# Seven raw weight tiles with nine loads ahead, and one set of activation buffers instead of two

## The chip, the cores and the metric

The kernel runs on one core of a Trainium2 chip. TensorE (PE) multiplies, VectorE (DVE) and ScalarE (ACT) work elementwise, SyncE (SP) issues nearly all DMA transfers, GpSimd (POOL) does little. The metric is the device time of one execution in microseconds (us); the time before is a median of three runs.

## What is computed

A decoder trunk of two layers over 256 tokens of width 2048, all in float32. The parts that matter here, from the reference:

```python
for layer in range(DEPTH):
    if layer % 2 == 0:
        mix = hybrid_mixer(rms_norm(x, ...), ...)     # state-space heads and stick-breaking attention
    else:
        mix = multiscale_pool(rms_norm(x, ...), ...)  # trailing means of 2/4/8/16 tokens, a map per group, bias, scale
    x = x + mix
    x = x + sq_relu_mlp(rms_norm(x, ...), mlp_w_up[layer], mlp_w_down[layer])

def sq_relu_mlp(h, w_up, w_down):
    u = jax.nn.relu(h @ w_up)
    return (u * u) @ w_down        # 2048 -> 8192 -> 2048
```

## The kernel before

**The list of weights.** `plan()` (L48) writes down all matrix products as units in a fixed order: the input projection of layer 0, its output projection, the MLP of layer 0, the four groups of the pooling layer, the MLP of layer 1. A unit is cut into steps; a step is one load of up to 512 KB of weights, two tiles of 128x512 or four of 128x256. The weights lie in device memory in the order of the steps.

**From load to matmul.** Each step goes through `load` (L198), which issues the DMA on SP's queue into a `raw` tile, and `split` (L215), in which ACT writes `hi`, the weights rounded to the matmul's float32r type (L235), and DVE writes `lo`, the rest (L236). A product is the sum of three matmuls: `hi` times the two halves of the activations, and `lo` times the high half. There are four `raw` tiles, four `hi` and four `lo`. `feed` (L239) keeps the loads six steps and the splits three steps ahead of the step whose matmuls are written next.

**The MLP.** It runs in four blocks of 2048 hidden columns. For block 0, eight `up` units make the squared activations `u`; for blocks 1 to 3, four `up` units make the first half of the columns, and the second half is made by two units, `sa` and `sb`, that use seven products for a two-by-two block product (Strassen's scheme). Their 20 steps are laid by `plan()` among the 32 steps of the `down` units of the block before, from due numbers (L94). For `sb`, DVE first combines the raw tiles of two steps in place (L222 to L225). The sums of activations that the seven products need, `sop`, are made by `gen_sop` (L691) once a layer, eight tiles of them, and are kept until the last `sb` of the layer. The seven products are added and squared in `gen_s` (L735), and the result is turned into place by `to_ring` (L286).

**Where things lie.** Fourteen slots of 8 KB per partition (`slot(i)`) hold normed inputs, mixer outputs, `u` and constants by turns. `u_base` (L788) says in which four slots a block's `u` lies; the blocks of a layer alternate between two sets. `t4` tiles, eight of them, hold short-lived work of the mixer and the pooling layer, and `sop`. The constants of the pooling layer (window matrix, bias, scale) are loaded in `finish` (L839 to L852) after the first `down` unit of the last block of layer 0, into slots 4 to 7, from SP's queue; the bias is added to the residual stream by `add_bias` (L761), and `gen_win` (L766) adds the pooled groups.

**The order.** The program is written in one order by the loop over steps and by small generators that are advanced a tick at a time (`lane`, `lane2`). The tile framework then orders each engine's instructions: it can move one ahead of its place in the program where its inputs and its tile are free, and a new tile of a name waits until the readers of the old one are through. On the chip each engine runs its own list in order.

Of the kernel before, what the change touches and what calls it, by code (L numbers as in the profile page):

```python
# [11 lines left out]
F32R = mybir.dt.float32r  # L12
# [4 lines left out]
P = 128  # L17
# [21 lines left out]


X_EARLY = ((0, 14), (1, 2), (1, 6), (1, 10))
AHEAD_LOAD = 6
WARM = 2
PAD, TURN = 24, 56
AHEAD_SPLIT = 3
# [83 lines left out]
def tile_trunk(ctx: ExitStack, tc: tile.TileContext, x_in, xt_in, w_all, prm_in,  # L129
# [11 lines left out]
    def new(tag, shape, dt=F32, bufs=1, p=sb):  # L141
        count[0] += 1
        return p.tile(shape, dt, tag=tag, name=f"{tag}_{count[0]}", bufs=bufs)

    def slot(i, shape=(P, 2, 4, T), dt=F32R):
        return new(f"st{i}", list(shape), dt)

    def ev():
        return new("ev", [P, MT, 512], bufs=3)

    def t4(n, dt=F32):
        return new("t4", [P, 1088], dt, bufs=8)[:, :n]

    def bank():
        return new("bg", [P, 512], bufs=4, p=ps_bg)
# [1 line left out]
    def v3(ap, a, b):  # L157
        return ap.rearrange("p (a b) -> p a b", a=a, b=b)
# [23 lines left out]
    def load_x(q):  # L182

        m, c = q // 2, slice(D // 2 * (q % 2), D // 2 * (q % 2) + D // 2)
        if q == 0:
            x_sb[:] = [slot(12 + m, (P, D), F32) for m in range(MT)]
        nc.sync.dma_start(x_sb[m][:, c], x_in[m * P : m * P + P, c])
# [10 lines left out]
    def load(i):  # L198
        u, k, tiles, off = steps[i]
        n, nk = units[u]["n"], len(tiles)  # L200
        raw = v3(new("raw", [P, 1024], bufs=4)[:, : nk * n], nk, n)
        if u == 0:
            nc.sync.dma_start(
                xt[k // 8][:, k % 8 : k % 8 + nk, :],
                xt_in[k * P : (k + nk) * P, :].rearrange("(k p) n -> p k n", p=P))
        nc.sync.dma_start(
            raw, w_all[off : off + P * nk * n].rearrange("(p k n) -> p k n", p=P, n=n))
        raws[i] = raw
        if u == 0 and k == 8:
            nc.sync.dma_start(cst, cst_in)  # L210
            nc.sync.dma_start(row, row_in.partition_broadcast(P))
        if (u, k) in X_EARLY:
            load_x(X_EARLY.index((u, k)))
# [25 lines left out]
    def feed(i):  # L239
        while done["load"] < min(len(steps), i + 1 + AHEAD_LOAD):  # L240
            load(done["load"])
            done["load"] += 1
        while done["split"] < min(len(steps), i + 1 + AHEAD_SPLIT):
            split(done["split"])
            done["split"] += 1
# [62 lines left out]
    def spread(name):  # L308

        r = rs[name]  # L310
        dg = v3(t4(2 * P), MT, P)
        for m in range(MT):
            dve.tensor_scalar(dg[:, m], ident, r[:, m : m + 1], None, ALU.mult)
        yield
        b = bank()
        for m in range(MT):
            pe.matmul(b[:, m * P : (m + 1) * P], ones, dg[:, m], start=True, stop=True)
        o = new("rrow", [P, T], bufs=2)
        dve.tensor_copy(o, b[:, :T])
        rs[name, "row"] = o  # L320
# [9 lines left out]
    def norm_chunk(name, c, tiles, slot0, gain):  # L330
        if c == 0:
            rs[name, "ss"] = new("ss", [P, MT, 4], bufs=2)
        ss = rs[name, "ss"]
        junk = t4(512)
        for m in range(MT):
            act.activation(junk, x_sb[m][:, 512 * c : 512 * c + 512], AF.Square,
                           accum_out=ss[:, m, c : c + 1])
        if c == 3:
            s = new("sum", [P, MT], bufs=2)
            dve.tensor_reduce(s, ss, AX.X, ALU.add)  # L340
            r = new("rstd", [P, MT], bufs=2)
            power(r, s, 1.0 / D)
            rs[name] = r
        yield
        yield
        dst = slot(slot0 + c)
        yield from to_ring(lambda m: x_sb[m][:, 512 * c : 512 * c + 512], tiles, 4 * c, dst, gain)
        if c == 3 and name != "pool":
            yield from spread(name)
# [10 lines left out]
    def turn(e, n):  # L360

        yield
        yield
        xT = v3(t4(n * 259), n, 259)
        for h in range(n // 2):
            b = v3(bank(), 2, T)
            for c in range(2):
                for m in range(MT):
                    k = 2 * h + c
                    pe.transpose(b[:, c, m * P : (m + 1) * P], e[:, m, k * P : (k + 1) * P], ident)  # L370
            act.activation(xT[:, 2 * h : 2 * h + 2, 3:], b, AF.Copy)
            yield
        return xT
# [317 lines left out]
    def gen_sop(layer):  # L691


        for p in range(KT // 2):
            t, c = hM[layer][2 * p]
            e = ev()
            a, s = v3(e[:, 0], 2, T), v3(e[:, 1], 4, P)
            dve.tensor_tensor(a, t[:, 0, c : c + 2].bitcast(F32), t[:, 1, c : c + 2].bitcast(F32),
                              ALU.add)
            a11, a21, a12, a22 = (a[:, i, h * P : h * P + P] for i in range(2) for h in range(2))  # L700
            dve.tensor_tensor(s[:, 0], a21, a22, ALU.add)
            dve.tensor_tensor(s[:, 2], a11, a21, ALU.subtract)
            dve.tensor_tensor(s[:, 1], s[:, 0], a11, ALU.subtract)
            dve.tensor_tensor(s[:, 3], a12, s[:, 1], ALU.subtract)
            yield
            o = t4(1024, F32R).rearrange("p (a b c) -> p a b c", a=2, b=4)
            act.activation(o[:, 0], s, AF.Copy)
            dve.tensor_tensor(o[:, 1], s, o[:, 0].bitcast(F32), ALU.subtract)
            sop[layer, p] = o
            yield  # L710
            yield
# [74 lines left out]
        yield  # L786

    def u_base(layer, b):  # L788
        return ((4, 8), (0, 4))[layer][b % 2]

    def finish(u, ps):
        d = units[u]
# [62 lines left out]
        elif kind == "pool":  # L855
            need(lambda: "pool" in rs)
            w = [v3(t4(1024, F32R), MT, 512) for _ in range(2)]
            r = rs["pool"]
            for m in range(MT):
                rm = r[:, m : m + 1]  # L860
                act.activation(w[0][:, m], ps[:, m], AF.Copy, scale=rm)
                dve.scalar_tensor_tensor(w[1][:, m], ps[:, m], rm, w[0][:, m].bitcast(F32),
                                         ALU.mult, ALU.subtract)
            lane.append(gen_win(arg, w))
        elif kind == "up":
            layer, b, i = arg
            name = f"mlp{layer}"
            need(lambda: (name, "row") in rs)
            e = ev()
            ea, eb = v3(e[:, 0], 2, T), v3(e[:, 1], 2, T)  # L870
            add_halves(ea, ps)
            dve.scalar_tensor_tensor(ea, ea, 0.0, row2(name), ALU.max, ALU.mult)
            lane.append(gen_u(b, i, ea, eb, u_base(layer, b)))
            if (b, i) == (0, 0):
                lane2.append(gen_sop(layer))
        elif kind == "sa":

            a = sev["a"] = new("att_b", [P, 3, 512])
            p1, p2, p3 = (sps.pop(q) for q in (1, 2, 3))
            act.activation(a[:, 2], p1, AF.Copy)  # L880
            act.activation(a[:, 1], p3, AF.Copy)
            dve.tensor_tensor(a[:, 0], a[:, 2], p2, ALU.add)
        elif kind == "sb":
            lane.append(gen_s(*arg, u_base(*arg)))
# [42 lines left out]
    for i, (u, k, tiles, _) in enumerate(steps):  # L927
        d = units[u]
        n, nk, src, k0, n2 = d["n"], d["nk"], sources[d["src"]], d["k0"], len(tiles)
# [10 lines left out]
        if u not in accs:  # L940
            accs[u] = ps_main.tile([P, MT, 512], F32, tag="acc", name=f"acc_{u}")
            if d["kind"] == "up" and d["arg"][2] == 0:
                b = d["arg"][1]
# [11 lines left out]
        for kk in range(n2):  # L955
            t, c = src[k0 + k + kk]
# [89 lines left out]
```

## Time and profile before

| what | before |
|---|---|
| median of three runs | 2184.68 us (2181.84 to 2185.71) |
| profiled execution, its own time | 2179.63 us |
| span of its instructions | 2177.8 us |
| PE busy, idle | 2160.8 us, 17.0 us |
| weight load on PE busy | 1816.5 us |
| DVE busy | 1552.5 us |
| ACT busy | 1191.5 us |
| moved by DMA | 454.32 MB, mean 209 GB/s |

Busy times are sums over the span; different stages have different limits, so they are read stage by stage. A matmul's end is modelled, and matmuls overlap, so the time between two starts says more than the time of one. A row of a group gives engine, operation, out<-in with sizes, count, then busy time and mean, then the idle time of the engine ahead of it and what ended it. A row of waits gives who waited for whom, the sum, the number and the longest.

### The profile page before, as it was taken

Reading aid. Unit: us, or ns where it says so; the run is one execution under the profiler, and the core shown is the slowest. Engines: PE = TensorE matmul, PEld = TensorE weight load, DVE = VectorE, ACT = ScalarE, POOL = GpSimd, SP = SyncE. Lnnn points to the kernel's source line nnn. Section 1 sums busy time; section 2 is a strip of 40 time slices with the busy share of each in tenths; the row PEclk is TensorE's granted clock in tenths of the full one; section 3 lists DMA queues with packets and bytes.
Section 4 is the critical chain, followed back from the end, with each engine's and each line's share of the span. In section 5 each row is a group of like instructions: output and inputs, shape, how many; then the busy total and the mean of one; then the engine's idle time right before and its main releaser. Section 6 shows DMA issues by size and latency. Waiting matters only on the chain.

```text
span 2177.8 us, 28400 instructions
## 1 busy us (share of the span) xinstructions
PE 2160.8 (99%) x10613; PEld 1816.5 (83%) x10613; DVE 1552.5 (71%) x1908; ACT 1191.5 (55%) x1399; POOL 21.5 (1%) x21
## 2 busy tenths in 40 slices
PE   9999999999999999999999999999999999999999
PEld 7888888888888888788878878888887887888888
DVE  6988756656555586886886787578778777768754
ACT  7665456665644465455455455456554654654543
POOL 0000000000000000000000000000000000000000
PEclk9999999999999999999999999999999999999999
DMA  8665555555656567766776776655677676677664
GB/s 303 202 205 165 165 184 163 176 165 172 205 187 190 176 200 239 225 230 220 239 240 206 247 257 232 184 174 162 207 242 240 204 250 231 215 242 232 222 202 146
DMA packets 129002, 454.32 MB, mean 209 GB/s; under 512 B 14496, under 2 KB 17248, under 8 KB 128608
## 3 DMA queue, kind: packets, MB, share of 16 engines
q1 hardware_dynamic: 128000, 451.36, 64.5%
q8 instruction: 83, 1.36, 0.3%
q10 hardware_dynamic: 864, 1.15, 0.2%
q14 instruction: 55, 0.45, 0.1%
HBM read 450.32 MB, written 2.13 MB: 208 GB/s over the span
## 4 chain that ended last, share of the span: by engine, by line
PE 89%; DMA 5%; DVE 4%; ACT 1%; issue 1%; DVEq 0%; ACTq 0%; SPq 0%
PE acc L969 52%; PE acc L961 16%; PE acc L963 9%; PE bg L732 8%; DMA raw<-w_all 5%; DVE lo L236 2%; PE bg L294 1%; ACT hi L235 1%; DVE raw L224 1%; DVE raw L223 1%; PE bg L522 1%; DVE raw L225 0%; PE bg L579 0%; PE bg L669 0%; PE bg L614 0%
## 5 line engine op out<-in xcount | busy, mean ns | idle before, releaser
L235 ACT ACTIVATE hi<-raw 128x1024 fp32r<-128x1024 f32 (+2 forms) x846 | 878.7, 1048 | 905.2 <-PE acc L969 442.6
L236 DVE TENSOR_TENSOR lo<-raw,hi 128x1024 fp32r<-128x1024 f32 (+2 forms) x846 | 1012.8, 1205 | 446.4 <-ACT hi L235 422.1
L969 PE MATMUL acc<-hi,st 128*128 128x512 f32 (+2 forms) x3840 | 1165.0, 386 | 1.8 <-ACT hi L235 1.8
L969 PEld LDWEIGHTS acc<-hi,st 128*128 128x128 f32 x3840 | 710.1, 188 | 142.9 <-ACT hi L235 3.7
L969 PE MATMUL acc<-lo,st 128*128 128x512 f32 (+2 forms) x1920 | 736.3, 385 | 1.3 <-DVE lo L236 1.1
L961 PE MATMUL acc<-st,hi 128*128 128x512 f32 x1568 | 552.3, 394 | 0.0
L963 PE MATMUL acc<-st,lo 128*128 128x256 f32 x1568 | 441.7, 282 | 0.0
L969 PEld LDWEIGHTS acc<-lo,st 128*128 128x128 f32 x1920 | 360.6, 188 | 75.6 <-DVE lo L236 3.3
L961 PEld LDWEIGHTS acc<-st,hi 128*128 128x128 f32 x1568 | 294.3, 188 | 62.0 <-issue 1.4
L963 PEld LDWEIGHTS acc<-st,lo 128*128 128x128 f32 x1568 | 296.3, 189 | 2.0 <-issue 1.2
L732 PE MATMUL bg<-hi,t 128*128 128x512 f32 x384 | 119.2, 392 | 0.0
L732 PE MATMUL bg<-hi,st 128*128 128x512 f32 x288 | 88.8, 390 | 0.0
L732 PE MATMUL bg<-lo,t 128*128 128x512 f32 x192 | 77.3, 403 | 8.1 <-DVE lo L236 8.1
L732 PEld LDWEIGHTS bg<-hi,t 128*128 128x128 f32 x384 | 71.3, 188 | 15.9 <-ACT hi L235 2.1
L222 DVE TENSOR_TENSOR raw<-raw 128x512 f32<-128x512 f32 x48 | 33.2, 692 | 45.2 <-DMA raw<-w_all 45.1
L732 PEld LDWEIGHTS bg<-hi,st 128*128 128x128 f32 x288 | 54.1, 188 | 10.4
L732 PEld LDWEIGHTS bg<-lo,t 128*128 128x128 f32 x192 | 36.0, 187 | 25.8 <-DVE lo L236 17.0
L832 DVE TENSOR_TENSOR st<-st,acc 128x512 f32<-128x512 f32 (+1 forms) x74 | 46.4, 668 | 13.8 <-PE acc L969 13.8
L732 PE MATMUL bg<-lo,st 128*128 128x512 f32 x144 | 56.0, 389 | 0.0
L223 DVE TENSOR_TENSOR raw<-raw,raw 128x512 f32<-128x512 f32 x48 | 33.2, 692 | 23.5 <-DMA raw<-w_all 23.3
L282 ACT ACTIVATE st<-bg,prm 128x256 fp32r<-128x256 f32 x64 | 28.4, 467 | 23.9 <-DVE st L283 22.8
L325 DVE TENSOR_TENSOR ev<-acc,ev 128x512 f32<-128x512 f32 x40 | 27.4, 685 | 11.6 <-ACT ev L324 11.6
(190 smaller groups left out, 1067.8 us busy)
## 6 DMA issues: line engine op xcount, KB each, us to landing
raw<-w_all SPq DMA_DIRECT2D x818, 512.0 KB, 3.9
raw<-w_all SPq DMA_DIRECT2D x20, 256.0 KB, 2.9
st<-x_in SPq DMA_DIRECT2D x8, 512.0 KB, 5.1
st<-scr SPq DMA_DIRECT2D x8, 512.0 KB, 6.6
raw<-w_all SPq DMA_DIRECT2D x8, 288.0 KB, 4.2
st<-prow_in SPq DMA_DIRECT2D x2, 1024.0 KB, 7.1
st<-xt_in SPq DMA_DIRECT2D x6, 256.0 KB, 6.9
st<-pmat_in SPq DMA_DIRECT2D x1, 768.0 KB, 7.0
```

What stands on the lines that cost most here:

```text
L222: dve.tensor_tensor(raw[:, 0], raw[:, 1], raw[:, 0], ALU.subtract)
L223: dve.tensor_tensor(raw[:, 1], two[:, 0], raw[:, 1], ALU.subtract)
L224: dve.tensor_tensor(two[:, 0], two[:, 0], raw[:, 0], ALU.subtract)
L235: act.activation(hi, raw, AF.Copy)
L236: dve.tensor_tensor(lo, raw, hi.bitcast(F32), ALU.subtract)
L282: act.activation(dst[:, 0, c], ps, AF.Copy, scale=gain)
L325: dve.tensor_tensor(dst, ps[:, :, :T], dst, ALU.add)
L732: pe.matmul(sps[q], st[h], w[:, j], start=p == 0 and w is hi and h == 0, stop=p == KT // 2 - 1 and w is lo)
L832: dve.tensor_tensor(x_sb[m][:, cs], x_sb[m][:, cs], ps[:, m, : d["n"]], ALU.add)
L961: pe.matmul(ps[:, f].rearrange("p (h t) -> p h t", h=2), hi[:, kk, fs], t[:, :, c], start=first, stop=False)
L963: pe.matmul(ps[:, f, :T], lo[:, kk, fs], t[:, 0, c], start=False, stop=last)
L969: pe.matmul(ps[:, m, :n], t[:, h % 2, c, m * P : (m + 1) * P], (hi, hi, lo)[h][:, kk], start=first and h == 0, stop=last and h == 2)
```

## The change

Four edits, in one diff:

- `raw` has seven tiles instead of four, and loads are written nine steps ahead instead of six.
- `t4` has five tiles of 1036 columns instead of eight of 1088.
- `sop` no longer takes a `t4` tile for each of its eight pairs; two pairs share one slot, slots 8 to 11 in layer 0 and 4 to 7 in layer 1.
- `u` lies in one set of four slots in all blocks of a layer, slots 4 to 7 in layer 0 and 0 to 3 in layer 1, where two sets alternated.

```diff
-AHEAD_LOAD = 6
+RAWS, AHEAD_LOAD = 7, 9
...
     def t4(n, dt=F32):
-        return new("t4", [P, 1088], dt, bufs=8)[:, :n]
+        return new("t4", [P, 1036], dt, bufs=5)[:, :n]
...
-        raw = v3(new("raw", [P, 1024], bufs=4)[:, : nk * n], nk, n)
+        raw = v3(new("raw", [P, 1024], bufs=RAWS)[:, : nk * n], nk, n)
...
-            o = t4(1024, F32R).rearrange("p (a b c) -> p a b c", a=2, b=4)
+            if p % 2 == 0:
+                dst = slot((8, 4)[layer] + p // 2, (P, 2, 2, 4, P))
+            o = dst[:, p % 2]
             act.activation(o[:, 0], s, AF.Copy)
...
     def u_base(layer, b):
-        return ((4, 8), (0, 4))[layer][b % 2]
+        return (4, 0)[layer]
```

## The prediction

> **What bounds the kernel now.** I read the page first (busy shares, costly groups), then the table of waits, then sums over stretches of time, then single instructions in two places.
>
> ```profile
> span 2177.8 us, 28400 instructions
> PE 2160.8 (99%) x10613; PEld 1816.5 (83%) x10613; DVE 1552.5 (71%) x1908; ACT 1191.5 (55%) x1399; POOL 21.5 (1%) x21
> raw<-w_all SPq DMA_DIRECT2D x818, 512.0 KB, 3.9
> ```
> TensorE (PE) has work in all but 17.0 us of the span. No edit here removes a matmul, so the most there is to win is these gaps and the little that a broken rhythm costs around them. Where they lie:
>
> ```profile
> 0.00:15.00 15.00, 11.70 (x37) 7.25 (x38) 8.46 (x16) 9.94 (x17) 0.31 (x5) 1.00 0.87 302
> 15.00:860.00 845.00, 845.00 (x4211) 714.64 (x4210) 571.36 (x801) 486.57 (x598) 19.82 (x14) 1.00 0.60 191
> 865.00:961.00 96.00, 93.81 (x412) 75.49 (x412) 77.78 (x86) 47.34 (x47) 0.00 (x0) 1.00 0.70 231
> 1040.00:1135.00 95.00, 93.76 (x414) 76.03 (x414) 78.02 (x86) 47.28 (x47) 0.00 (x0) 1.00 0.70 234
> 1214.00:1308.00 94.00, 92.96 (x413) 75.96 (x412) 78.18 (x87) 47.67 (x47) 0.00 (x0) 1.00 0.75 252
> 1600.00:1694.00 94.00, 92.67 (x409) 75.03 (x408) 77.17 (x86) 46.73 (x47) 0.00 (x0) 1.00 0.72 237
> 1773.00:1869.00 96.00, 94.37 (x416) 76.46 (x415) 78.82 (x88) 47.32 (x48) 0.00 (x0) 1.00 0.70 234
> 1948.00:2044.00 96.00, 94.08 (x418) 76.64 (x417) 78.75 (x88) 47.91 (x48) 0.00 (x0) 1.00 0.72 233
> 1418.00:1440.00 22.00, 22.00 (x102) 18.20 (x101) 13.60 (x16) 10.98 (x16) 0.00 (x0) 1.00 0.59 188
> 1440.00:1452.00 12.00, 12.00 (x58) 10.03 (x57) 10.08 (x16) 8.34 (x14) 0.70 (x1) 1.00 0.52 179
> 1452.00:1475.00 23.00, 22.43 (x109) 18.02 (x108) 21.90 (x32) 16.03 (x31) 0.00 (x0) 1.00 0.46 142
> ```
> The first pair of columns is the stretch and its length, then busy time of PE, weight load, DVE, ACT and POOL, the granted clock, the DMA share and GB/s. From 15 to 860 us (mixer of layer 0, its first `up` units) PE has no idle time at all. The start has 3.3 us. The six stretches from 865 on are the `down` units of blocks 0 to 2 of both layers, with the seven-product (Strassen) units `sa` and `sb` laid between them; they have 2.19 + 1.24 + 1.04 + 1.33 + 1.63 + 1.92 = 9.35 us idle. Who is late there:
>
> ```profile
> SPq L206 <- DVE lo L236: 1713.6, 805, 7.1
> DVE raw L222 <- DMA raw<-w_all: 45.1, 42, 2.8
> DVE raw L223 <- DMA raw<-w_all: 23.3, 39, 2.0
> PEld bg L732 <- DVE lo L236: 17.0, 22, 1.1
> ```
> ```profile
> 910.69 0.69 DVE L222 TENSOR_TENSOR raw<-raw 128x512 f32<-128x512 f32 x1 [0.99 <-DMA raw<-w_all]
> 911.30 1.22 DVE L236 TENSOR_TENSOR lo<-raw,hi 128x1024 fp32r<-128x1024 f32 x1
> 913.05 0.69 DVE L223 TENSOR_TENSOR raw<-raw,raw 128x512 f32<-128x512 f32 x1 [0.54 <-DMA raw<-w_all]
> 915.12 3.71 DVE L236 TENSOR_TENSOR lo<-raw,hi 128x1024 fp32r<-128x1024 f32 x3
> 915.14 0.63 PE L732 MATMUL bg<-hi,t 128*128 128x512 f32 x2
> 916.39 0.50 PE L732 MATMUL bg<-lo,t 128*128 128x512 f32 x1 [0.62 <-DVE lo L236]
> 916.72 0.63 PE L732 MATMUL bg<-hi,t 128*128 128x512 f32 x2
> 1682.53 8.17 PE acc L969 x36
> ```
> This is one `sb` pair. DVE must combine two raw tiles (L222 to L225) before it can make `lo`. It waits 0.99 us for the first tile, which holds back the `lo` behind it in DVE's order, and 0.54 us for the second; 1.5 us later than need be, `lo` releases PE. The loads are late because SP, which issues them, nearly always waits for a `raw` tile to be given back by `lo` (805 times), and a load needs 3.9 us from issue to landing.
>
> **The change part by part.** *Seven raw tiles, nine loads ahead.* No instruction is added; the loads stay the same. A load can be issued when the tile seven places back is given back instead of four. Three loads earlier is at least 4.1 us of lead (36 matmuls take 8.17 us, so one takes 0.227 and an `sb` step of six 1.36; three steps). That is more than the longest of these DMA waits, 2.8 us. DMA can deliver: 231 to 252 GB/s flow in these stretches, 302 at the start. One stall costs more than the idle time shown: the `lo` matmul should have begun at 915.14 + 2 x 0.227 = 915.59 and began at 916.39 (0.80 late), and the next followed after 0.33 instead of 0.227 (0.10 more): 0.90 us for 0.62 idle. On 9.35 us that makes 13.6 us, the upper bound. The lower is nothing, if DVE's own order keeps `lo` late. I take 11.5: DVE is busy 78 of 96 us there, so it has room to catch up, but only four `hi` and `lo` tiles remain, so it can run ahead by L222 to L225 alone, and a close pair may still be late. At the start the DMA share is already 0.87 of 16 engines over the first 15 us, so a deeper queue brings little there: I take 0 (bounds 0 and the 3.3 us gained).
>
> The Trainium skill (Perfetto Trace Analysis, "Optimization Strategy") says that the same gap repeating on the engine that should be saturated can mean that there is too little SBUF for the next tile. By it the whole 13.6 us would come back, by the row of DVE's load 11.5; no run here shows yet which.
>
> *Five t4 tiles instead of eight.* In the MLP the eight products' operands (`sop`) held all eight; they move out, so five remain for the rest. Most are needed in the pool stage:
>
> ```profile
> 1455.09 0.74 DVE L782 SCALAR_TENSOR_TENSOR t<-bg,cnt,st 128x512 f32<-128x512 f32 x1
> 1455.20 0.63 ACT L336 ACTIVATE t<-st 128x512 f32<-128x512 f32 x1 [2.13 <-DVE st L784]
> 1455.83 0.67 ACT L861 ACTIVATE t<-acc,rstd 128x512 fp32r<-128x512 f32 x1
> 1455.86 0.69 DVE L784 TENSOR_TENSOR st<-st,t 128x512 f32<-128x512 f32 x1
> 1456.54 0.75 DVE L862 SCALAR_TENSOR_TENSOR t<-acc,rstd,t 128x512 fp32r<-128x512 f32 x1
> ```
> Two for `w` (L861, L862), one for the squares (L336), up to two for `t` (L782, L784): five at once. Cost 0; bounds 0 and 0.75 (one L782 waiting for another) per pool group, 3.0 in all.
>
> *`sop` into slots, one set of four slots for `u`.* The writes of `sop` are the same instructions. The next block's `u` now goes into the slots that the `down` units still read. Its first writer (L279, from the combined Strassen products) comes after transposes that PE runs itself, behind the last `down` matmul, so no new wait: 0, with PE's own order as the cover; if that were gone, the wait is one `down` unit's tail.
>
> *What the diff does not mention: the pool constants.* They are loaded into slots 4 to 7. So far block 3 of layer 0 kept its `u` in 8 to 11 and these were free from block 2 on. Now block 3 sits in 4 to 7 until its last `down` unit has read them.
>
> ```profile
> L848 SPq DMA_DIRECT2D st<-prow_in x2: 423/425/427, 1287.3 to 1307.6; - x2
> DMA to landing us min/median/max: 6.6/7.1/7.5
> L852 DVE TENSOR_TENSOR st<-st,st x4: 681/684/691, 1315.2 to 1318.8; 128x512 f32<-128x512 f32 x4
> L763 DVE TENSOR_TENSOR st<-st,st x8: 680/682/696, 1383.9 to 1447.3; 128x512 f32<-128x512 f32 x8
> L843 ACT ACTIVATE st<-st x1: 1488/1488/1488, 1309.7 to 1309.7; 128x1536 fp32r<-128x1536 f32 x1
> L774 PE MATMUL bg<-t,st x8: 389/389/501, 1452.0 to 1472.2; 128*128 128x512 f32 x8
> L782 DVE SCALAR_TENSOR_TENSOR t<-bg,cnt,st x8: 742/746/750, 1452.7 to 1476.8; 128x512 f32<-128x512 f32 x8
> 1302.59 0.38 SPq L841 DMA_DIRECT2D st<-pmat_in  x1
> 1467.96 0.39 PE L961 MATMUL acc<-st,hi 128*128 128x512 f32 x1
> ```
> The last `down` unit runs from 1418 to 1440 and reads four tiles of `u`, a slot, in a quarter of that, 5.5 us: slots 4, 5, 6, 7 come free at 1423.5, 1429, 1434.5, 1440. Bias, scale and window matrix can land 7.1 us later, at 1430.6, 1436.1 and 1441.6 at the earliest. The matrix is then copied (L843, 1.5 us) by 1443, before its first use at 1452 (L774): no cost. The slots are read until 1476.8 (L782); `sop` of layer 1 takes them after the first `up` unit, which begins at 1467.96 and holds 32 long matmuls (7.3 us) and 32 short ones: at worst a microsecond's wait, counted 0. What is late next is DVE: four products (L852, 2.7 us) and the first six of eight bias additions (L763, 4.1 us; the last two are in the stage already) move from covered places into the pool stage, which must end in the normed input of `up` at 1467.96. DVE's room: 3.9 us of the 22 before 1440 that lie after 1436.1, at its 38% idle, 1.5; then 1.9 up to 1452 and 1.1 up to 1475. So 6.8 - 4.5 = 2.3 us late is the low bound. If scale is again issued 20.3 us after bias (1287.3, 1307.6), though its slot is free, it lands near 1454; then 2.7 + 5.5 = 8.2 us of DVE work stands before 1475 with 1.0 us of room: 7.2 us late, the high bound. PE has nothing else to do then, so DVE's delay is PE's. I take 4.5, the middle, since the order of SP's queue in the new program is not in this trace.
>
> **Sum.** -11.5 + 0 + 0 + 0 + 4.5 = -7.0 us, on the profiled execution's own 2179.6 (span 2177.8) 2172.6. The median of the runs is 2184.7, 5 us above that execution; on it the forecast is **2177.7**.
>
> **Rivals.** *Bubbles go wholly and the constants come early:* -13.6 + 2.3 = -11.3, 2173.4. For it: DMA waits are in nearly every pair (42 of 48), PE stalls in fewer. Against: the four `hi` and `lo` tiles.
>
> *DVE's order, not the loads, is the limit:* only the stalls that directly follow a long DMA wait go, some 4 us, and the stage costs 4.5: 2185. For it: DVE's pair costs 4 x 0.69 + 4 x 1.22 = 7.6 us against 8.2 of PE work (12 matmuls for the pair, 24 for two `down` steps); against it: 1.5 us of that pair's time is shown as DMA wait.
>
> *Slower: the constants jam SP and DVE.* SP issues in order. If scale stands in its queue behind loads that wait for tiles which DVE gives back, it lands later than 1454, and each microsecond costs PE one. Gain and cost are even at a landing near 1458 (7.2 + 4.3 = 11.5); from 1463 on the kernel is slower by more than can be told from no change. At 1465 the cost is 18, the time 2191. For it: seven loads, not four, may stand ahead, and scale came late before. Against: PE's idle time there is only 0.57 us now, and loads flow at 142 GB/s, so SP is not crowded.
>
> By the Trainium skill (TensorE: Matmul & The Clock Gate, "HAM oscillation") a PE gap over some 3.4 us halves its clock until it has been busy that long again; in this rival that would add about 1.7 us (3.4 us at half speed). The granted clock is 1.00 in all rows above, with no idle gap as long, so the trace can't say.
>
> **How the numbers follow.** Chances: forecast 40, bubbles wholly gone 25, DVE's order 22, jam 13. A measurement of this kernel tells apart some 0.2%, 4.4 us. Faster: 33 of the forecast's 40 (its own range is 2173 to 2182), all 25: 58. Same: 7 and 17 of DVE's order, 1 of the jam: 25. Slower: 5 and 12: 17. The range takes in the early constants with the whole gain and 3 us of spread between runs (2170) and, above, 5 us gained with 7.2 lost (2187); that leaves most of the jam out.
>
> **What would show it.** Waits of L222 and L223 for `raw` fall from 68 us to under 20 and those of the weight load L732 for `lo` from 17.0 to under 4, or the first step is wrong. Idle PE in the six stretches under 3 us. L848 and L841 issue after the last `down` unit has begun, L852 runs after 1430 and PE shows 2 to 7 us of idle between the last pool matmul and the first of `up`. PE idle anywhere in 15 to 860 us would mean that five t4 tiles are too few, and the forecast is wrong if that, or the gap before `up`, is over 11 us.

## The result, and the profile after

The changed kernel takes 2165.03 us (median of four runs, 2163.73 to 2166.34), the kernel before 2183.92: ratio 0.9914, 95% interval 0.9897 to 0.9931. That is 18.9 us faster; 7.0 were forecast, and the stated range ended at 2170. By the two profiled executions it is 14.8 us (spans 2177.8 and 2163.0).

The first lines of the page after, then its rows of waits for the same pairs as before (lines have moved by two from L706 on, so L971 answers to L969, L734 to L732):

```profile
span 2163.0 us, 28389 instructions
PE 2154.4 (100%) x10613; PEld 1820.6 (84%) x10613; DVE 1541.7 (71%) x1908; ACT 1203.2 (56%) x1401; POOL 21.7 (1%) x21
...
raw<-w_all SPq DMA_DIRECT2D x818, 512.0 KB, 3.8
```
```profile
SPq L206 <- DVE lo L236: 1678.5, 790, 7.2
DVE raw L222 <- DMA raw<-w_all: 31.0, 23, 3.2
DVE raw L223 <- DMA raw<-w_all: 19.9, 25, 2.8
PEld acc L971 <- DVE lo L236: 2.2, 6, 0.7
```
PE's idle time fell from 17.0 to 8.6 us. The weight load of L734 no longer waits for `lo` at all (17.0 us before). But DVE still waits 51 us for loads of pairs, where it waited 68: most of these waits did not go, they ceased to hold PE up. That is the first sign that "loads come earlier" is not the whole cause. (A pair is two neighbouring steps of `sb`, whose raw tiles DVE combines; L222 needs the first load, L223 the second. An `sb` unit has eight pairs, the kernel 48. With the twelve steps of `sa` a block lays 28 steps in 20 places among the `down` steps.)

Sums over stretches of the changed kernel (the columns are those of the prediction's table):

```profile
15.00:860.00 845.00, 844.75 (x4211) 714.48 (x4210) 570.82 (x801) 488.26 (x599) 19.97 (x14) 1.00 0.60 193
860.00:1310.00 450.00, 449.69 (x2142) 378.61 (x2141) 347.65 (x377) 246.43 (x254) 0.00 (x0) 1.00 0.72 236
1436.00:1468.00 32.00, 30.20 (x145) 24.10 (x145) 30.82 (x47) 22.10 (x43) 0.70 (x1) 1.00 0.56 173
1595.00:2045.00 450.00, 450.00 (x2155) 378.84 (x2154) 347.60 (x377) 247.78 (x257) 0.00 (x0) 1.00 0.72 235
```
The two stretches of 450 us hold all six that the prediction summed: 0.31 us idle is left of 9.35. The mixer is as fast as before, so five t4 tiles are enough there: its 0.25 us of idle time is one wait of a matmul (L490) for ACT, and kernels with eight t4 tiles have such idle time too (0.14 us in the second trace of the kernel before, 0.50 with the ordering described below). The pool stage (1436 to 1468) now idles 1.8 us.

A ledger comes out of the starts of the matmuls, 10613 in both traces. This is the start of the n-th matmul after, less that of the n-th before:

```
n-th matmul      4300   4800   5200   5600   6200   6900   7200   8000   9000  10000  10612
before, us      872.1  980.8 1064.5 1150.5 1279.8 1421.8 1483.1 1639.6 1856.6 2062.5 2173.7
after - before   -0.1   -4.0   -4.0   -6.7   -8.1   -8.0   -6.4   -6.4  -11.7  -14.8  -14.8
```
Nothing is won up to 872 us, 8.0 in the first three stretches, 8.4 in the last three, and 1.6 is given back in the pool stage between 1422 and 1483. So 16.4 us came from 9.0 us of idle time: a stall costs 1.8 times its visible idle time. Sorted by matmul, 12.5 of the 16.4 us lie at the 19 matmuls of these stretches that had idle time ahead of them, 2.1 at the matmul behind each of those, and 1.8 are spread over the other 4144.

### The profile page after: what moved, and what is told of

It reads as the page before. It is cut to its first block, busy times and chain, and to the rows that moved or that the text cites. A ratio compares the mean times of both kernels' runs of the same rounds, so it can differ in the third digit from the quotient of the medians.

```text
span 2163.0 us, 28389 instructions
## 1 busy us (share of the span) xinstructions
PE 2154.4 (100%) x10613; PEld 1820.6 (84%) x10613; DVE 1541.7 (71%) x1908; ACT 1203.2 (56%) x1401; POOL 21.7 (1%) x21
## 4 chain that ended last, share of the span: by engine, by line
PE 97%; DVE 1%; DMA 1%; issue 0%; ACT 0%; SPq 0%; DVEq 0%; ACTq 0%
PE acc L971 58%; PE acc L963 16%; PE bg L734 10%; PE acc L965 9%; PE bg L294 1%; PE bg L522 1%; DVE lo L236 0%; DMA raw<-w_all 0%; PE bg L579 0%; PE bg L669 0%; PE bg L614 0%; DMA st<-prow_in 0%; DVE st L765 0%; PE bg L610 0%; PE bg L671 0%
## 5 line engine op out<-in xcount | busy, mean ns | idle before, releaser
L235 ACT ACTIVATE hi<-raw 128x1024 fp32r<-128x1024 f32 (+2 forms) x846 | 887.6, 1049 | 889.8 <-PE acc L971 586.2
L971 PE MATMUL acc<-hi,st 128*128 128x512 f32 (+2 forms) x3840 | 1165.6, 386 | 0.9 <-ACT hi L235 0.9
L971 PEld LDWEIGHTS acc<-hi,st 128*128 128x128 f32 x3840 | 710.9, 188 | 142.1 <-ACT hi L235 2.4
L971 PE MATMUL acc<-lo,st 128*128 128x512 f32 (+2 forms) x1920 | 736.2, 385 | 0.4 <-DVE lo L236 0.3
L971 PEld LDWEIGHTS acc<-lo,st 128*128 128x128 f32 x1920 | 360.6, 188 | 74.1 <-DVE lo L236 2.2
L734 PE MATMUL bg<-hi,st 128*128 128x512 f32 x672 | 206.9, 389 | 0.0
L734 PEld LDWEIGHTS bg<-hi,st 128*128 128x128 f32 x672 | 126.1, 188 | 26.3
L734 PE MATMUL bg<-lo,st 128*128 128x512 f32 x336 | 130.7, 389 | 0.0
L734 PEld LDWEIGHTS bg<-lo,st 128*128 128x128 f32 x336 | 63.1, 188 | 13.0
L834 DVE TENSOR_TENSOR st<-st,acc 128x512 f32<-128x512 f32 (+1 forms) x74 | 46.4, 669 | 15.9 <-PE acc L971 15.6
L222 DVE TENSOR_TENSOR raw<-raw 128x512 f32<-128x512 f32 x48 | 33.1, 689 | 31.1 <-DMA raw<-w_all 31.0
L223 DVE TENSOR_TENSOR raw<-raw,raw 128x512 f32<-128x512 f32 x48 | 33.1, 690 | 20.7 <-DMA raw<-w_all 19.9
L283 DVE SCALAR_TENSOR_TENSOR st<-bg,prm,st 128x256 fp32r<-128x256 f32 x64 | 29.5, 481 | 8.2 <-ACT st L282 8.2
L225 DVE TENSOR_TENSOR raw<-raw 128x512 f32<-128x512 f32 x48 | 33.1, 690 | 1.0
L224 DVE TENSOR_TENSOR raw<-raw,raw 128x512 f32<-128x512 f32 x48 | 32.9, 686 | 0.2
```

Source lines behind the costliest of these rows:

```text
L222: dve.tensor_tensor(raw[:, 0], raw[:, 1], raw[:, 0], ALU.subtract)
L223: dve.tensor_tensor(raw[:, 1], two[:, 0], raw[:, 1], ALU.subtract)
L224: dve.tensor_tensor(two[:, 0], two[:, 0], raw[:, 0], ALU.subtract)
L225: dve.tensor_tensor(two[:, 1], two[:, 0], two[:, 1], ALU.subtract)
L235: act.activation(hi, raw, AF.Copy)
L283: dve.scalar_tensor_tensor(dst[:, 1, c], ps, gain, dst[:, 0, c].bitcast(F32), ALU.mult, ALU.subtract)
```

## The experiments

Times are medians; ratios are to the kernel before, run on the same chip in the same job. Its median was 2183.3 us in the job with the second trace, four and five tiles and the early constants, 2185.5 in that with six tiles and the ordering, and 2184.2 in that with the loads six ahead and "best"; so times of different jobs are compared by their ratios. "Idle" is PE's idle time in the two stretches of 450 us, from these rows (kernel before, its second trace, four, five, six tiles, and five tiles with the ordering, in this order):

```profile
860.00:1310.00 450.00, 445.53 (x2093) 369.47 (x2093) 346.90 (x371) 236.86 (x248) 0.00 (x0) 1.00 0.71 235
1595.00:2045.00 450.00, 445.12 (x2092) 369.28 (x2091) 347.16 (x370) 236.75 (x248) 0.00 (x0) 1.00 0.71 231
```
```profile
860.00:1310.00 450.00, 445.48 (x2094) 370.00 (x2093) 347.25 (x371) 237.19 (x247) 0.00 (x0) 1.00 0.71 235
1595.00:2045.00 450.00, 446.20 (x2099) 370.80 (x2099) 348.06 (x372) 238.46 (x249) 0.00 (x0) 1.00 0.71 232
```
```profile
860.00:1310.00 450.00, 443.67 (x2077) 366.97 (x2076) 344.68 (x368) 234.35 (x245) 0.00 (x0) 1.00 0.70 230
1595.00:2045.00 450.00, 443.81 (x2073) 366.77 (x2072) 343.06 (x364) 233.04 (x243) 0.00 (x0) 1.00 0.70 231
```
```profile
860.00:1310.00 450.00, 443.23 (x2076) 367.75 (x2075) 343.69 (x371) 238.58 (x247) 0.00 (x0) 1.00 0.70 232
1595.00:2045.00 450.00, 446.08 (x2095) 371.46 (x2094) 345.66 (x373) 241.03 (x250) 0.00 (x0) 1.00 0.70 234
```
```profile
860.00:1310.00 450.00, 445.08 (x2093) 370.40 (x2092) 344.24 (x372) 241.44 (x249) 0.00 (x0) 1.00 0.72 233
1595.00:2045.00 450.00, 444.67 (x2090) 370.51 (x2090) 344.24 (x372) 242.23 (x248) 0.00 (x0) 1.00 0.72 233
```
```profile
860.00:1310.00 450.00, 450.00 (x2144) 379.26 (x2143) 352.73 (x376) 245.51 (x254) 0.00 (x0) 1.00 0.72 237
1595.00:2045.00 450.00, 450.00 (x2158) 379.80 (x2157) 353.59 (x378) 245.78 (x258) 0.00 (x0) 1.00 0.72 234
```

| kernel | raw tiles | median us | ratio, 95% interval | time of the profiled execution, its idle |
|---|---|---|---|---|
| before | 4 | 2183.9 | 1 | 2179.6, 9.35 |
| before, again | 4 | 2183.95 | 1.000 (0.9991 to 1.0010) | 2178.6, 8.32 |
| new layout | 4 | 2186.3 | 1.0013 (1.0004 to 1.0022) | 2187.1, 12.52 |
| new layout | 5 | 2185.9 | 1.0015 (1.0005 to 1.0026) | 2182.6, 10.69 |
| new layout | 6 | 2182.5 | 0.9981 (0.9972 to 0.9991) | 2182.5, 10.25 |
| changed kernel | 7 | 2165.0 | 0.9914 (0.9897 to 0.9931) | 2164.8, 0.31 |
| seven tiles, loads six ahead | 7 | 2166.4 | 0.9919 (0.9904 to 0.9934) | 2165.6, 0.57 |
| before with the ordering | 4 | 2186.8 | 1.0008 (0.9999 to 1.0016) | 2185.5, 12.73 |
| new layout with the ordering | 5 | 2164.6 | 0.9905 (0.9890 to 0.9920) | 2164.3, 0.00 |
| changed kernel with the ordering | 7 | 2164.6 | 0.9903 (0.9890 to 0.9917) | 2164.2, 0.00 |
| changed kernel, constants early | 7 | 2163.5 | 0.9911 (0.9898 to 0.9925) | 2163.7, 0.00 |
| both, "best" | 7 | 2162.4 | 0.9900 (0.9883 to 0.9916) | 2161.7, 0.00 |

**The kernel before once more.** No edit.

> The kernel before, once more, for a second trace of it. The gain was 18.9 us by the medians but 14.8 us by the two profiled spans, so 4 us are not in the first trace. Theory A (late loads): how long the loads take to land varies from run to run, the profiled execution of before was a light one, and the idle time of PE in the six stretches with the seven-product units grows with the run's own time: 9.4 us at 2179.6, and about 0.7 us more for each us of run time above that (one stall cost 0.90 us for 0.62 idle), so some 12 us at 2183.5; no idle time elsewhere. Rival B: the 4 us are something else, and a second trace of a 2183 us execution shows again 9 to 10 us idle in the six stretches. Time by both: 2184, ratio 1.000 within 0.001.

Its eleven runs spread from 2178.6 to 2186.8, and the profiled one was the fastest of them, as it was in the first set (2179.6 against 2181.8 to 2185.7). So the second trace does not show a 2184 us execution and can't decide A against B by itself. The traces of the next kernels do: at 2187.1, 2182.6, 2182.5 and 2185.5 us the idle time is 12.5, 10.7, 10.3 and 12.7 us. Time rises with this idle time by about 1.8 us per us, as in the ledger; at 1.8, the 4 us by which the median of before lies above its profiled execution are an estimated 2.4 us more idle time, some 12 us in all. That step is by analogy: no trace of before at 2184 was had, nor did the traces show what makes one run of it heavier than the next.

**The layout alone.**

```diff
-RAWS, AHEAD_LOAD = 7, 9
+RAWS, AHEAD_LOAD = 4, 6
```


> The changed kernel with the four raw tiles and six loads ahead of before: only the new layout (five t4 tiles, products' operands in slots, one set for the squared activations, constants after the last down unit has begun). Theory A: all of the gain is the loads' lead, so this is no faster than before: 2184 to 2186, ratio 1.000 to 1.001, with 9 to 13 us idle on PE in the six stretches and 1 to 2 us more than before at the pool stage. Rival B: the layout, by the new order of instructions or the operands' new places, brings 4 to 5 us itself: 2179 to 2180, ratio 0.998.

2186.3, 0.13% slower than before: rival B falls. The new places, five t4 tiles and the single set of `u` bring nothing and cost 2 to 3 us. Of these the pool stage can account for 1.5 to 2.0 (2.0 by the starts of this kernel's matmuls). The parts of the layout were not run one by one.

**Five and six tiles.**

```diff
-RAWS, AHEAD_LOAD = 7, 9
+RAWS, AHEAD_LOAD = 5, 7      # and 6, 8
```


> The changed kernel with five raw tiles and seven loads ahead. Theory A: one load earlier is 1.4 to 2.7 us of lead, the mean DMA wait of the first combining instruction was 1.07 us and the longest 2.8, so most stalls go: 2168 to 2174, with 1 to 4 us idle in the six stretches. Rival B (DVE's own order keeps lo late unless it can combine tiles far ahead): half of the gain at most, 2175 to 2180.

2185.9, against 2186.3 with four tiles in the same job: one more tile brings nothing. This was the surprise of the study, and both theories missed it. The rows of waits with five tiles:

```profile
DVE raw L222 <- DMA raw<-w_all: 66.4, 41, 3.0
DVE raw L223 <- DMA raw<-w_all: 10.2, 19, 1.6
PEld acc L971 <- DVE lo L236: 20.5, 27, 1.7
PEld bg L734 <- DVE lo L236: 2.4, 3, 1.5
```
The second tile of a pair is now mostly in time (10.2 us of waits, 23.3 before), and the products of the pair no longer wait (2.4, before 17.0). In their place the ordinary `down` steps wait 20.5 us for `lo`, which was 3 us before. The instructions show why; DVE, then PE:

```profile
919.60 0.69 DVE L222 TENSOR_TENSOR raw<-raw 128x512 f32<-128x512 f32 x1 [2.77 <-DMA raw<-w_all]
920.21 1.22 DVE L236 TENSOR_TENSOR lo<-raw,hi 128x1024 fp32r<-128x1024 f32 x1
```
```profile
920.00 0.61 PE L971 MATMUL acc<-hi,st 128*128 128x512 f32 x2
921.49 0.50 PE L971 MATMUL acc<-lo,st 128*128 128x512 f32 x1 [0.88 <-DVE lo L236]
```
L222 stands in DVE's queue ahead of the `lo` of the two steps before it, although it comes later in the program; the planner (the tile framework's ordering) moved it forward. Its load, issued at 914.59, lands at 919.51; DVE stands still for 2.77 us, and PE waits for the `lo` behind it, whose own weights had landed at 913.83. So a theory A2 was formed: DVE's order, not the load, makes PE wait.

> The changed kernel with six raw tiles and eight loads ahead. With four tiles the new layout took 2186.3, with five 2185.9, with seven 2165.0. Theory A2 (DVE's queue order: the first combining instruction, L222, is placed where the planner believes its load has landed, the real load lands 1 to 3 us later, and DVE's next lo waits behind it; tiles help only when the lo products are far enough ahead of PE to bear that wait, which is a threshold and not a slope): six tiles are past it for most pairs, 2166 to 2172. Theory A (lead of the loads alone, with a gain for every load of lead): two thirds of the way from five to seven, 2171 to 2174, which after the run with five tiles is already doubtful.

2182.5: six tiles give 3 us, where A2 had forecast 2166 to 2172 and A 2171 to 2174. Its rows of waits:

```profile
DVE raw L222 <- DMA raw<-w_all: 58.1, 41, 3.0
DVE raw L223 <- DMA raw<-w_all: 20.6, 29, 1.8
PEld acc L971 <- DVE lo L236: 21.8, 27, 1.8
```
DVE's waits for pairs are as long as ever (79 us), and 27 weight loads of L971 still wait 21.8 us for `lo`.

Why an added tile brings so little stands in the order of DVE's rows. With four tiles L222 is ahead of one `lo` that comes before it in the program (in 42 of the 48 pairs; of none in 6), with five ahead of two (of three in 6), with six ahead of three (of two in 6). The load of a step can go out when the `lo` as many steps back as there are raw tiles has given its tile back. Between that `lo` and L222, DVE so has two others to do, in these 42 pairs of each kernel: the planner spends every added tile on placing L222 one `lo` earlier, and L222 still comes upon a load that is under way (45.1, 66.4 and 58.1 us of waits in the kernel before and with five and six tiles), with one more `lo` behind it each time.

**The order mended, tiles as before, five and seven.** L222 is put behind the `lo` of the step before it in DVE's queue. That is an order within one engine: in the traces with and without it the queues of SP and PE hold the same instructions in the same order, and with four tiles only DVE's differs. (The runs with five and seven tiles have the new layout, that with four is the kernel before.)

```diff
+            with tc.issue_after(lo_ins[0]):     # lo of the step before
-            dve.tensor_tensor(raw[:, 0], raw[:, 1], raw[:, 0], ALU.subtract)
+                dve.tensor_tensor(raw[:, 0], raw[:, 1], raw[:, 0], ALU.subtract)
```


> The kernel before (four raw tiles), with one ordering added: L222 of each pair must stand behind the lo of the step before it in DVE's queue, where the planner had put it ahead. No load is issued earlier. Theory A (late loads): nothing is gained, 2182 to 2186, since the pair's second load still ends the wait; the idle time of PE in the stretches stays 9 us and over. Theory A2 (DVE's order): the lo of the down step is no longer held, but with four tiles it was mostly the pair's own lo that was late (0.48 us ahead of PE in the median), so only a part goes: 2177 to 2181.

> Five raw tiles with seven loads ahead, and L222 behind the lo of the step before. In the run with five tiles without this ordering, the pairs' lo had gained lead (2.25 us in the median against 0.48), but PE waited 27 times for the lo of a down step that stood behind a waiting L222. Theory A2: with the order mended five tiles give most of the gain, 2166 to 2172, with under 3 us idle in the stretches. Theory A (only the loads' lead counts, five are too few): 2183 to 2186 as without it.

> The changed kernel (seven tiles), with L222 behind the lo of the step before. Both theories: 2164 to 2166, nothing to win, since PE loses under 1 us in the stretches; the DVE waits of L222 and L223 for loads, 51 us in the changed kernel, fall to under 15 by A2, as they come from L222 being placed early and not from loads that PE needs.

With four tiles 2186.8 (nothing, perhaps a loss), with five 2164.6, with seven 2164.6. The stretches with four tiles and the ordering, 12.73 us idle together:

```profile
860.00:1310.00 450.00, 443.07 (x2072) 365.89 (x2071) 343.58 (x368) 233.51 (x245) 0.00 (x0) 1.00 0.72 232
1595.00:2045.00 450.00, 444.20 (x2074) 367.01 (x2073) 342.87 (x365) 231.59 (x243) 0.00 (x0) 1.00 0.70 230
```
Waits for loads with four tiles and the ordering (lines have moved by two: L225 is the second combining instruction, L238 is `lo`), then with five:

```profile
DVE raw L225 <- DMA raw<-w_all: 52.0, 39, 3.0
PEld bg L734 <- DVE lo L238: 22.6, 26, 1.1
```
```profile
DVE raw L225 <- DMA raw<-w_all: 3.1, 4, 1.4
```
With four tiles, DVE waits 52 us for the pair's *second* load in place of the first; the load itself is late, and this order does not help. With five tiles and the right order only 3.1 us of DVE's waits for loads are left in the whole kernel, and PE idles nowhere in the stretches. A pair of it on DVE (L224 is the first combining instruction here):

```profile
908.74 1.23 DVE L238 TENSOR_TENSOR lo<-raw,hi 128x1024 fp32r<-128x1024 f32 x1 [0.61 <-ACT hi L237]
909.88 0.68 DVE L224 TENSOR_TENSOR raw<-raw 128x512 f32<-128x512 f32 x1
```
So two things were needed together, one tile more and an order in which DVE does not stand before a load that is under way. Either alone is worth nothing: 2185.9 and 2186.8. With seven tiles the ordering takes away DVE's waits for loads (51 us before it) and leaves the time as it was, as both theories said.

**Seven tiles, loads written six ahead.**

```diff
-RAWS, AHEAD_LOAD = 7, 9
+RAWS, AHEAD_LOAD = 7, 6
```


> Seven raw tiles, but loads written only six steps ahead in the program, as before. The planner moves loads up to where a tile is free, so if the tiles count and not the place in the program, this is the changed kernel: 2164 to 2167, ratio 0.991 to before. If the nine loads ahead matter (the planner ranks instructions by their place in the program, and L222 of a pair would move with them), DVE's order changes and stalls come back: 2172 to 2184.

2166.4, ratio 0.9919 to the 0.9914 of the changed kernel, with intervals that overlap: the gain is the tiles. The two traces show why nine loads ahead add nothing that can be told: every engine has its instructions in the same order, but for two weight loads in the first third of SP's queue that change places with other DMAs.

**The pool constants early.**

```diff
     def u_base(layer, b):
-        return (4, 0)[layer]
+        return 8 if (layer, b) == (0, NB - 1) else (4, 0)[layer]
```


> The changed kernel, but the squared activations of the last block of layer 0 lie in slots 8 to 11 (free after the last product of the seven), so that the pool constants can be loaded a block earlier, as in the kernel before. In the trace of the changed kernel PE loses 2.3 us between 1436 and 1468 us, where before lost 0.8. Theory A: the late constants cost that difference: 2163.5, ratio to the changed kernel 0.9993. Rival: the pool stage is limited by DVE either way, and the new order costs it as much: 2165, nothing gained.

2163.5, as forecast by theory A, but the medians alone don't decide it (0.9911 and 0.9914 of the kernel before, with intervals that overlap). The ledger of starts does: this kernel stands 7.1 us ahead of the kernel before on entering the pool stage and 7.0 on leaving it, where the changed kernel gives back 1.6.

**All three.** The ordering and the early constants on top of the changed kernel.

> Three things together: seven raw tiles, L222 behind the lo of the step before, and the squared activations of layer 0's last block in slots 8 to 11, so that the pool constants load a block earlier. The stretches have nothing left to give (under 1 us), the pool stage 1.5 us as measured alone: 2163 to 2164, 1 to 2 us under the changed kernel, ratio 0.9995 to 0.999 to it. If the constants' place and the ordering disturb each other, 2165 or more.

2162.4 (2161.65 to 2162.91): the fastest of the study, and its four runs lie below all four of the changed kernel; they are of different jobs, and the intervals of the two ratios overlap. The expectation was missed to the good side by 0.6 us.

## Why the prediction was wrong

**What bounds the kernel: right.** All of the gain lies in the six stretches, none in the mixer or at the start, as the table of stretches had said.

**The sum: three terms were mis-sized.** From the forecast 7.0 us to the measured 18.9 it is 4.9 us in the stalls (16.4 for 11.5), 2.9 in the constants (1.6 for 4.5), and 4.1 that the two profiled executions do not show (18.9 for 14.8).

**The size of the stalls.** The step "on 9.35 us that makes 13.6 us, the upper bound" measured one stall (0.90 us for 0.62 idle) and carried its factor to all. The ledger gives 16.4 us for 9.0, so the bound was no bound. By the ledger sorted by matmul, the stalled matmuls and those right behind them, which is what that factor counts, make 14.6 us of it, for 13.6: the factor was nearly right. The other 1.8 us lie where PE shows no idle time; the starts should have been summed, not one stall. And the sum was made on a profiled execution, then set on a median 5 us above it. Those 5 us were taken for an offset; they were, by the analogy above, more of the same stalls, so they were to be won as well. Taking 11.5 of 13.6 was too careful: 0.31 us idle was left. The condition of its lower bound, "if DVE's own order keeps `lo` late", is what happens with five and six tiles; with seven it no longer costs PE time.

**The cause of the stalls: half right, and the test in the prediction said so.** It asked for the waits of L222 and L223 to "fall from 68 us to under 20", and they fell to 51; the other half of it, the weight load's waits for `lo` under 4 us, came true. The step "three loads earlier is at least 4.1 us of lead ... more than the longest of these DMA waits" treated each tile as lead that L222 keeps. Five tiles refute that, since one more tile gained nothing. What holds: with four tiles the second load of a pair is late (the ordering alone did not help); with five and six PE hardly waits for the pair's own `lo` any more (2.4 us with five, no such row with six), but DVE stands before the first load, and the harm moves to the `lo` of the `down` steps. With seven tiles L222 is ahead of three `lo` in 24 of the pairs, of four in 12 and of five in 12. In the 24, three others lie between the `lo` that gives the tile back and L222, one more than before, and L222 never waits there; in the other 24 it waits 23 times, 31.0 us in all. One of each, with a wait and without:

```profile
908.56 0.69 DVE L222 TENSOR_TENSOR raw<-raw 128x512 f32<-128x512 f32 x1 [1.05 <-DMA raw<-w_all]
929.78 0.68 DVE L222 TENSOR_TENSOR raw<-raw 128x512 f32<-128x512 f32 x1
```
And `lo` is further ahead of PE: that of the second step before a pair ends 2.35 us ahead of its first matmul in the median, where it was 0.68 with six tiles, so weight loads wait only 2.2 us for `lo` where they waited 21.8. By these rows the step between six and seven comes with the planner's placing; no run changed that placing alone with six tiles, and why the planner places L222 as it does is not shown. Nor did any run give more `hi` and `lo` tiles, which the prediction held against a full gain. The rival "DVE's order, not the loads, is the limit" had the second half of the cause, with the wrong time: it was to leave the kernel at 2185, which is where five tiles stand, and seven tiles step over it.

**The Trainium skill's rule** on repeating gaps (Perfetto Trace Analysis, "Optimization Strategy") would have brought the whole of the gap back, and at seven tiles it did. At five tiles, though, the same gaps stood beside one more tile, and they went by an ordering; the rule names a possible cause, and the run decides. The Trainium skill's rule on the clock gate (TensorE: Matmul & The Clock Gate, "HAM oscillation") met no case here: the longest idle gap of PE in the changed kernel is 1.45 us, and the granted clock stays at 1.00 in all rows above.

**The pool constants: found rightly, priced too high.** 4.5 us was taken between 2.3 and 7.2; the cost was 1.6 by the starts, 1.5 by the medians. The issue and the work on them, from the lines of the changed kernel:

```profile
L850 SPq DMA_DIRECT2D st<-prow_in x2: 327/328/328, 1415.1 to 1421.0; - x2
L843 SPq DMA_DIRECT2D st<-pmat_in x1: 328/328/328, 1426.9 to 1426.9; - x1
1427.71 2.50 DVE L854 TENSOR_TENSOR st<-st,st 128x512 f32<-128x512 f32 x4 [1.34 <-DMA st<-prow_in]
1430.13 3.70 DVE L765 TENSOR_TENSOR st<-st,st 128x512 f32<-128x512 f32 x6
1436.01 1.28 DVE L834 TENSOR_TENSOR st<-st,acc 128x512 f32<-128x512 f32 x2
```
The loads went out 6 us apart, as the slots came free, and the 20 us between bias and scale did not recur: the low bound was the case. (The high bound had a slip as well: 20.3 us after a landing at 1430.6 is 1450.9, not 1454.) The low bound's own price was too high by 0.7. The step that failed is "DVE's delay is PE's": the last `down` sum (L834) came about 4 us later against its matmuls than before, but PE had pool matmuls to do meanwhile. Its 1.8 us of idle time fall into three gaps ahead of pool matmuls or of the transposes before them, where 2 to 7 us in one gap ahead of `up` had been expected. The jam rival did not come up.

**t4, `sop`, the single set: right** as far as PE in the mixer and at the blocks' joints shows; no run changed one of them alone. The layout together is 0.13% slower (some 3 us), of which the constants are half or more.

## What to carry to other kernels

Look in the trace for an instruction that waits for a load while work whose inputs are there stands behind it on the same engine; an ordering edge there may be worth more than buffers (five tiles and an edge equal seven here), and buffers without it can show nothing where the planner spends them on placing the waiting instruction earlier. So count, after adding a buffer, how much ready work stands behind it. Sum what a stall costs from the starts of the instructions, not from idle time, and ask whether the profiled run is a light one before its stalls are used as the bound. When a buffer set is dropped, list everything that is loaded into its places.

## What had not been expected

Time as a function of the raw tiles is a step: 2186.3, 2185.9, 2182.5, 2165.0 us for four to seven (1.0013, 1.0015, 0.9981 and 0.9914 of the kernel before). And the spread seems to go with the stalls: 27 runs of the kernel before, in one job, lay between 2180.0 and 2190.2, eleven with five tiles between 2182.6 and 2192.1, while with five tiles and the ordering four runs lay within 1.9 us (2164.3 to 2166.2); four runs are few to set against eleven and 27.
